# Rotary scores as two packed fp32r products, and casts moved behind head outputs

## The chip, the cores and the metric

The kernel runs on one core of a Trainium2 chip. The metric is the device time of one execution in microseconds (us), lower is better. A run of this kernel is compared with a run of the kernel before on the same chip. A profile of one execution tells what each engine did: TensorE (PE, with its weight loads shown apart as PEld), VectorE (DVE), ScalarE (ACT), GpSimd (POOL) and the DMA queues, most of which are issued by SyncE (SP).

## The reference

The program is a two-layer streaming encoder over 256 positions of width 1024, all in fp32. Each layer adds half a SwiGLU feed-forward (hidden width 2816), a token mixer, and half a second feed-forward. The mixer of layer 0 is a Conformer convolution, that of layer 1 is latent attention with 8 heads. The change touches the attention and, in three of the four feed-forwards, an order on two engines. What the attention computes:

```python
s = (jnp.einsum("bqhd,bkhd->bhqk", q_nope[:, q0:q1], k_nope[:, :q1])      # 128 numbers a head
     + jnp.einsum("bqhr,bkr->bhqk", q_rope[:, q0:q1], k_rope[:, :q1])     # 64 numbers, one key for all heads
     ) * scale
s = jnp.where(mask[None, None], s, -jnp.inf)                              # chunks of 64 positions
p = jax.nn.softmax(s, axis=-1)
outs.append(jnp.einsum("bhqk,bkhd->bqhd", p, v[:, :q1]))                  # blocks of 128 queries
```

So the first 128 queries see 128 keys and the last 128 queries see 256.

## The kernel before, in words

Positions are two tiles of 128 (`tb` or `qb`, 0 and 1). Nearly all weights pass through one pipeline: a block of 128 x 2048 fp32 numbers is fetched by SP into one of 4 `raw` buffers, ACT casts it to the shorter fp32r type (`hi`), DVE subtracts to get the rest (`lo`), in two pieces of 1024 columns each, and the pair stands in one of 5 weight buffers until PE has used it. A product is then three fp32r matmuls (`mm3`, lines 330 to 336): high by low, high by high, low by high. A few products are single fp32 matmuls instead, among them the scores, the transposes and probabilities by values; PE executes each of these as two records, except for a transpose, which is one.

The program is written as a list of operations, and a planner gives each engine its order from estimated times. Where the author wants another order, `order(a, b)` places `a` behind `b` without a wait of its own, `urgent` gives operations priority and records them, and `behind` places casts of weights behind the last few urgent operations of their engine. Each engine executes its list strictly in order.

The attention (`mla_in`, from line 1424) goes in this order: low-rank projections; the queries' rotary part (`qr`, lines 1529 to 1550), which DVE rotates into `qrope` with temporaries `rp`; the first four heads' query part `QN` (line 1552); transposes of the rotated key `kd` and of `qrope` (lines 1553 to 1562), whose results are copied into `KR` and `QR`; all heads' keys `KN`; the values `VV` (24 matmuls named `v`); the scores of heads 0, 1 and 2; the second four heads' `QN`; then a loop in which a head's scores (PE), softmax (DVE and ACT), transpose of its probabilities (PE, copied to `ptT` by ACT), its product with the values (`pv`, one PSUM bank) and its split into `Oh` (ACT) and `Ol` (DVE, both in `evicted`) overlap with the output projection `o`. The key is kept twice along the partitions, in two halves of 64, so that even and odd heads can share one tile; the 64 free rows of `KR` and `QR` hold -1e30 and 1 in such places that their product is the chunk mask. So the scores of a head are, for each of the two query tiles,

```python
nc.tensor.matmul(sc[qb], QN[:, hd, tbs(qb)], KN[:, hd, :n], start=True, stop=False)
last = nc.tensor.matmul(sc[qb], QR[:, hd % 2, hd // 2, tbs(qb)], KR[:, hd % 2, :n], start=False, stop=True)
```

with n = 128 or 256. The weights that are cast during the heads are the four blocks `wo` of the output projection and the first blocks `in_f2w` of the feed-forward that follows.

In a feed-forward, hidden columns are worked out in chunks `c` of 512; each ends in two groups (one for each position tile) whose result `s` is turned by way of DRAM (`turn`, line 846: DVE transposes `gt`, SP writes `gd` and reads it back into `rows` or `gb`) and split into `Gh` (ACT) and `Gl` (DVE); the pairs of these two casts are listed in `gates`. In the second, third and fourth feed-forward, chunk 3 is worked out with seven block products instead of eight (`seven_products`, line 368). Its seven weight blocks are made from four fetched ones by four DVE subtractions of 128 x 2048 (`load_seven`, line 189), and lines 395 to 404 say where the casts of the last two groups (those of chunk 2) stand among the casts of these blocks.

Of the kernel before, what the change touches and what calls it, by code (L numbers as in the profile page):

```python
# [11 lines left out]
F32 = mybir.dt.float32  # L12
# [77 lines left out]
def trunk(ctx: ExitStack, tc: tile.TileContext, x, xt, first, pos, invf, gfin, wdw,  # L90
# [71 lines left out]


    casts = {}

    turns = []
    last_read = [None]
# [21 lines left out]
    def load_seven(j, four, b, pieces):  # L189
        hi = wp.tile([P, HB], F32R, tag="hi", name=uid("hi"))  # L190
        lo = wp.tile([P, HB], F32R, tag="lo", name=uid("lo"))
        n = len(loaded)
        if j == 0:
            b[11], b[12] = fetched(four[0]), fetched(four[1])
        elif j == 1:
            b[22] = fetched(four[3])
        elif j == 2:
            b[21] = fetched(four[2])
        def sub(out, left, right):
            ins = nc.vector.tensor_sub(out, left, right)  # L200
            behind(ins)
            return ins

        if j == 1:
            sub(b[11], b[12], b[11])
            sub(b[12], b[22], b[12])
        elif j == 2:
            sub(b[11], b[22], b[11])
        elif j == 6:
            sub(b[11], b[21], b[11])  # L210
        raw = b[(11, 11, 11, 21, 12, 22, 11)[j]]
        for i in range(pieces):
# [155 lines left out]
    def seven_products(xh, xl, forms, banks, late={}):  # L368
# [22 lines left out]
        last = urgent(nc.scalar.copy)(kept, c22)  # L391
# [1011 lines left out]
    def rope(pool, dst, src, n, cc, sn, tb, after=()):  # L1403

        w = n * 64
        t1, t2 = (pool.tile([P, w], F32, tag=f"rp{w}", name=uid("rp"), bufs=3 if n > 1 else 4) for _ in range(2))
        a = t1[:, :w].rearrange("p (n i f) -> p n i f", i=2, f=32)
        b = t2[:, :w].rearrange("p (n i f) -> p n i f", i=2, f=32)
        full = [P, n, 2, 32]
        turned = [nc.vector.tensor_tensor(a, src, cc[:, tb, :, :].unsqueeze(1).to_broadcast(full), op=ALU.mult)]  # L1410
        for i in range(2):
            turned.append(nc.vector.tensor_tensor(b[:, :, i, :], src[:, :, 1 - i, :],
                                                  sn[:, tb, i, :].unsqueeze(1).to_broadcast([P, n, 32]), op=ALU.mult))
        for ins in turned:
            for first in after:
                order(ins, first.ins)
        nc.vector.tensor_add(dst, t1[:, :w], t2[:, :w])
# [6 lines left out]
    def mla_in(act, X, make_next, cc, sn):  # L1424
# [4 lines left out]
        CKl = act.tile([P, 2, S], F32R, tag="CKl", name="CKl")  # L1429


        KR = act.tile([P, 2, S], F32, tag="KR", name="KR")
        QR = act.tile([P, 2, H // 2, S], F32, tag="QR", name="QR")
        for x, fill in ((KR, -1e30), (QR, 1.0)):
            nc.gpsimd.memset(x, 0.0)
            for parity in range(2):
                for tb in range(NT):
                    row = 64 * (1 - parity) + 32 * tb
                    t = tb * P + (CHUNK if x is KR else 0)
                    nc.gpsimd.memset(x[row:row + 1, parity, ..., t:t + CHUNK], fill)  # L1440

        last_low = [None]

# [132 lines left out]

        score_last, maxima, powers, scaled = [], [], [], []

        def scores(hd):
            b = bank("B", "sc")  # L1580
            sc = {0: b[:, :P], 1: b[:, P:P + S]}
            for qb in range(NT):
                n = (qb + 1) * P
                nc.tensor.matmul(sc[qb], QN[:, hd, tbs(qb)], KN[:, hd, :n], start=True, stop=False)
                last = nc.tensor.matmul(sc[qb], QR[:, hd % 2, hd // 2, tbs(qb)], KR[:, hd % 2, :n], start=False,
                                        stop=True)
            score_last.append(last)
            return softmax(sc)

# [19 lines left out]
        def probs(pr):  # L1609
            b = transposed(pr, 0, 3)  # L1610
            pt = act.tile([P, 3 * P], F32, tag="ptT", name=uid("ptT"), bufs=2)
            nc.scalar.copy(pt, b[:, :3 * P])
            return pt

        def evicted(hd, b):
            nc.scalar.copy(Oh[:, hd, :], b[:, :S])
            nc.vector.tensor_sub(Ol[:, hd, :], b[:, :S], Oh[:, hd, :].bitcast(F32))

        def values(hd, pt):
            b = bank("C", "pv")  # L1620
            nc.tensor.matmul(b[:, :S], VV[:, 0, hd * VH:(hd + 1) * VH], pt[:, :S], start=True, stop=False)
            nc.tensor.matmul(b[:, P:S], VV[:, 1, hd * VH:(hd + 1) * VH], pt[:, S:], start=False, stop=True)
# [18 lines left out]
        nope(part, QN, 4, CQh, CQl, 512, 4, (0, 4), score_last[-1:])  # L1641
        o = Rows(Oh, Ol, H)
        for i in range(2, H + 3):
# [175 lines left out]
```

## Time and profile before

| what | value |
|---|---|
| median of 3 runs | 896.05 us (895.89 to 896.4) |
| the profiled execution | 896.07 us, its span 894.3 us |
| PE busy | 886.9 us, 99% of the span |
| PE weight loads | 745.9 us, 83% |
| DVE busy | 743.1 us, 83% |
| ACT busy | 571.8 us, 64% |
| POOL busy | 104.2 us, 12% |
| granted TensorE clock | 0.999 |
| matmul records of the scores | 64 in all, started between 666.3 and 691.6 us |

In the rows of the timeline the columns are start, length, engine, line, operation, tiles written and read, shape, and a count where equal instructions are merged; a bracket tells the idle time of the engine before it. The length of a matmul reaches over the start of the next, since matmuls are pipelined; the distance from one start to the next is what a matmul costs on PE.

### The profile page before, as it was taken

How to read it: one execution, taken by the hardware profiler on the slowest of the kernel's cores; microseconds unless marked ns; L12 is line 12 of the kernel's file. 1: busy time of each engine (PE TensorE's matmuls, PEld its weight loads, DVE VectorE, ACT ScalarE, POOL GpSimd, SP SyncE). 2: the span in 40 equal slices, each digit the busy share in tenths (PEclk: the TensorE clock that was granted, in tenths of full speed). 3: DMA queues.
4: the chain of work that ended last, by engine and by line, in shares of the span. 5: the costliest groups of instructions: out<-in, count | busy, mean ns of one | idle time of the engine just before them, and what ended most of it. 6: DMA issues, size and time to landing. Idle time of an engine off the chain costs nothing.

```text
span 894.3 us, 12241 instructions
## 1 busy us (share of the span) xinstructions
PE 886.9 (99%) x4221; PEld 745.9 (83%) x4221; DVE 743.1 (83%) x1083; ACT 571.8 (64%) x993; POOL 104.2 (12%) x227
## 2 busy tenths in 40 slices
PE   9999999999999999999999999999999999999997
PEld 7888888898988888888888888888899888888886
DVE  6787789579998999999588989995768579989973
ACT  7966458488886646667375566673677566474752
POOL 1000000069962000000010000001400010000000
PEclk9999999999999999999999999999999999999999
DMA  9987629834215864939759369495635349378541
GB/s 330 375 303 274 232 59 355 295 121 172 106 60 194 289 258 144 374 109 388 259 175 339 118 218 357 123 392 182 223 142 189 141 154 342 104 260 317 180 196 48
DMA packets 71055, 198.94 MB, mean 222 GB/s; under 512 B 12369, under 2 KB 41937, under 8 KB 51665
## 3 DMA queue, kind: packets, MB, share of 16 engines
q1 hardware_dynamic: 70560, 197.47, 61.8%
q8 instruction: 33, 0.54, 0.2%
q10 hardware_dynamic: 432, 0.69, 0.2%
q14 instruction: 30, 0.24, 0.1%
HBM read 181.87 MB, written 16.25 MB: 222 GB/s over the span
## 4 chain that ended last, share of the span: by engine, by line
PE 92%; DVE 4%; ACT 2%; DMA 1%; issue 0%; SPq 0%; POOL 0%; DVEq 0%; ACTq 0%
PE u L336 16%; PE u L335 16%; PE u L332 16%; PE o L335 9%; PE o L336 9%; PE o L332 9%; PE gate L1005 2%; PE u L411 2%; DVE acc L1094 2%; PE u L1005 2%; PE tp L446 1%; PE a L335 1%; PE a L332 1%; PE a L336 1%; PE nope L336 1%; PE nope L332 1%
## 5 line engine op out<-in xcount | busy, mean ns | idle before, releaser
L247 DVE TENSOR_TENSOR lo<-raw,hi 128x1024 fp32r<-128x1024 f32 (+1 forms) x236 | 276.2, 1212 | 38.8 <-ACT hi L246 37.6
L246 ACT CAST hi<-raw 128x1024 fp32r<-128x1024 f32 (+1 forms) x238 | 236.8, 1044 | 89.3 <-DMA raw<-in_f2w 30.8
L332 PE MATMUL u<-lo,Xh 128*128 128x512 f32 x612 | 238.4, 389 | 0.1
L336 PE MATMUL u<-hi,Xl 128*128 128x512 f32 x612 | 238.3, 389 | 0.0
L335 PE MATMUL u<-hi,Xh 128*128 128x512 f32 x612 | 238.1, 389 | 0.0
L332 PEld LDWEIGHTS u<-lo,Xh 128*128 128x128 f32 x612 | 114.9, 188 | 24.5 <-ACT Xh L598 0.5
L336 PEld LDWEIGHTS u<-hi,Xl 128*128 128x128 f32 x612 | 114.9, 188 | 24.3 <-DVE Xl L465 0.5
L335 PEld LDWEIGHTS u<-hi,Xh 128*128 128x128 f32 x612 | 114.9, 188 | 23.8
L214 ACT CAST hi<-raw 128x1024 fp32r<-128x1024 f32 x98 | 97.7, 1050 | 51.8 <-DVE raw L200 44.9
L200 DVE TENSOR_TENSOR lo<-raw,hi 128x1024 fp32r<-128x1024 f32 x98 | 115.6, 1216 | 7.1 <-ACT hi L214 7.1
L332 PE MATMUL o<-lo,Gh 128*128 128x512 f32 (+1 forms) x276 | 106.6, 386 | 0.0
L335 PE MATMUL o<-hi,Gh 128*128 128x512 f32 (+1 forms) x276 | 106.5, 386 | 0.0
L336 PE MATMUL o<-hi,Gl 128*128 128x512 f32 (+1 forms) x276 | 106.5, 386 | 0.0
L437 POOL TENSOR_TENSOR ms<-ss 128x1 f32<-128x1 f32 x16 | 8.1, 510 | 597.6 <-ACT junk L429 597.6
L200 DVE TENSOR_TENSOR raw<-raw,raw 128x2048 f32<-128x2048 f32 x28 | 63.9, 2283 | 1.8 <-DMA raw<-in_f2w 0.9
L332 PEld LDWEIGHTS o<-lo,Gh 128*128 128x128 f32 x276 | 51.8, 188 | 10.5
L335 PEld LDWEIGHTS o<-hi,Gh 128*128 128x128 f32 x276 | 51.9, 188 | 10.5
L336 PEld LDWEIGHTS o<-hi,Gl 128*128 128x128 f32 x276 | 51.8, 188 | 10.4
L1094 DVE SCALAR_TENSOR_TENSOR acc<-V,dw,acc 128x128 f32<-128x128 f32 (+1 forms) x174 | 53.9, 391 | 0.0
L1115 ACT ACTIVATE prod<-V,dw 128x128 f32<-128x128 f32 (+1 forms) x128 | 45.6, 415 | 1.8 <-POOL Y L1116 1.0
L956 ACT ACTIVATE s<-u,R 128x512 f32<-128x512 f32 (+1 forms) x48 | 30.9, 647 | 24.8 <-PE u L336 24.1
L797 DVE SCALAR_TENSOR_TENSOR h<-o,rh,h 128x512 f32<-128x512 f32 (+1 forms) x18 | 12.9, 719 | 29.2 <-PE o L336 29.2
(265 smaller groups left out, 1257.7 us busy)
## 6 DMA issues: line engine op xcount, KB each, us to landing
raw<-in_f2w SPq DMA_DIRECT2D x66, 1024.0 KB, 6.2
raw<-in_f1w SPq DMA_DIRECT2D x62, 1024.0 KB, 6.5
raw<-in_cw SPq DMA_DIRECT2D x12, 1024.0 KB, 5.5
gd<-gt SPq DMA_DIRECT2D x160, 64.0 KB, 3.0
gb<-gd SPq DMA_DIRECT2D x24, 256.0 KB, 2.8
rows<-gd SPq DMA_DIRECT2D x16, 256.0 KB, 4.4
raw<-in_wo SPq DMA_DIRECT2D x4, 1024.0 KB, 4.9
hd<-rows SPq DMA_DIRECT2D x56, 64.0 KB, 2.4
```

The source lines that it names most:

```text
L200: ins = nc.vector.tensor_sub(out, left, right)
L214: casts[n, i] = nc.scalar.copy(hi[:, c], raw[:, c]), sub(lo[:, c], raw[:, c], hi[:, c].bitcast(F32))
L246: casts[len(loaded), i] = (nc.scalar.copy(hi[:, c], raw[:, c]), low.tensor_sub(lo[:, c], raw[:, c], hi[:, c].bitcast(F32)))
L247: low.tensor_sub(lo[:, c], raw[:, c], hi[:, c].bitcast(F32)))
L332: mm = nc.tensor.matmul(o, ah, bl, start=start, stop=False, skip_group_check=seeded)
L335: nc.tensor.matmul(o, ah, bh, start=False, stop=False, skip_group_check=seeded)
L336: return nc.tensor.matmul(o, al, bh, start=False, stop=stop, skip_group_check=seeded)
L411: mm = nc.tensor.matmul(o, al if kind == "x" else ah, bl if kind == "l" else bh, start=start and n == 0, stop=stop and n == len(kinds) - 1)
L956: nc.scalar.activation(s[:, :w], u[0, tb][:, :w], AF.Silu, scale=X.r[tb])
L1005: mm = nc.tensor.matmul(u[:, t], w[:, c], X.x[:, k, t], start=(k == 0), stop=(k == KT - 1))
L1094: dve_last.append(nc.vector.scalar_tensor_tensor(out if j == j1 - 1 else y, v, w, y, op0=ALU.mult, op1=ALU.add))
L1115: prods_last.append(nc.scalar.activation(p, v, AF.Copy, scale=w))
```

## The change

- **Scores.** The rotary part is no longer one fp32 matmul but two fp32r matmuls. The key is cast to fp32r in `KA` (both halves), its rest goes to `KR`. The queries' high part stays in `QR`; a new tile `QA` for each parity and position tile holds the high part in one half and the rest in the other. `QA` by `KA` gives high by high and rest by high in one product; `QR` by `KR` gives high by rest, and the mask. The `QN` by `KN` product stays fp32. For the second query tile it is moved behind the fp32r ones, and all six are chained.
- **Making them.** For the key, 4 copies on ACT (64 x 128) become 2 copies on ACT (128 x 128) and 4 subtractions on DVE (64 x 128). For the queries, 2 copies on ACT and 2 on DVE (64 x 512) become 4 copies on ACT, 4 subtractions and 4 copies on DVE. The tiles of `QA` share the 6 buffers (before 3) of the rotation's temporaries. The products `v` are placed behind the transposes of `qrope`: those of the first output behind the first four transposes, the others behind the second four. The load of ACT's exponential table is placed behind the last copy into `QR`.
- **Casts during the heads.** The high casts of `wo` block 1 move from behind the third softmax to behind the first two copies into `ptT`; the casts of `wo` blocks 2 and 3 and of the next block are placed behind `Oh` and `Ol` of heads 1, 2 and 3; head 2's `evicted` becomes urgent.
- **Gates.** In `seven_products` the low casts of chunk 1's groups are placed behind the subtraction of the third of the seven blocks, and chunk 2's groups go later: their high casts behind those of the sixth and seventh block, their low casts behind the last low cast of the next plain block.

```diff
-            sub(b[11], b[22], b[11])
+            thirds[n] = sub(b[11], b[22], b[11])
...
-        for high, low in gates[-NT:] if not late else ():
-            order(high, last.ins)
-            order(low, add.ins)
-        low_gates = [low for high, low in gates[-NT:] if not late]
+        for high, low in gates[-2 * NT:-NT] if not late else ():
+            order(low, thirds[n0 + 2].ins)
+        late_gates = gates[-NT:] if not late else ()
...
-        for low in low_gates[1:]:
-            order(low, casts[n0 + 6, PIECES - 1][1].ins)
+        for n, (high, low) in enumerate(late_gates):
+            order(high, casts[n0 + 5 + n, PIECES - 1][0].ins)
+            order(low, casts[n0 + 7, PIECES - 1][1].ins)
...
-        t1, t2 = (pool.tile([P, w], F32, tag=f"rp{w}", name=uid("rp"), bufs=3 if n > 1 else 4) for _ in range(2))
+        t1, t2 = (pool.tile([P, w], F32, tag=f"rp{w}", name=uid("rp"), bufs=6 if n > 1 else 4) for _ in range(2))
...
+            nc.scalar.copy(KA[:, tbs(t)], b[:, :P])
             for i in range(2):
                 half = slice(64 * i, 64 * i + 64)
-                nc.scalar.copy(KR[half, i, tbs(t)], b[half, :P])
+                nc.vector.tensor_sub(KR[half, i, tbs(t)], b[half, :P], KA[half, tbs(t)].bitcast(F32))
+        turns_of = [], []
         for tb in range(NT):
-            b = transposed(qr[tb], 0, 4, (last,)).rearrange("p (j t) -> p j t", t=P)
-            for parity, copy in ((0, nc.scalar.copy), (1, nc.vector.tensor_copy)):
-                half = slice(64 * parity, 64 * parity + 64)
-                urgent(copy)(QR[half, parity, :, tbs(tb)], b[half])
+            b = transposed(qr[tb], 0, 4, (last,), turns_of[tb]).rearrange("p (j t) -> p j t", t=P)
+            for parity in range(2):
+                half, rest = (slice(64 * i, 64 * i + 64) for i in (parity, 1 - parity))
+                high = QR[half, parity, :, tbs(tb)]
+                turned_last = urgent(nc.scalar.copy)(high, b[half])
+                both = act.tile([P, 512], F32R, tag="rp512", name=uid("QA"), bufs=6).rearrange("p (j t) -> p j t", t=P)
+                urgent(nc.vector.tensor_sub)(both[rest], b[half], high.bitcast(F32))
+                urgent(nc.vector.tensor_copy)(both[half], high)
+                QA[parity, tb] = both
...
-                    mm3(b, CKh[:, k, tbs(tb)], CKl[:, k, tbs(tb)], hi[:, c], lo[:, c], k == 0, k == 1)
+                    mm3(b, CKh[:, k, tbs(tb)], CKl[:, k, tbs(tb)], hi[:, c], lo[:, c], k == 0, k == 1,
+                        turns_of[0][-1:] if (tb, d) == (0, 0) else turns_of[1][-1:])
...
-                nc.tensor.matmul(sc[qb], QN[:, hd, tbs(qb)], KN[:, hd, :n], start=True, stop=False)
-                last = nc.tensor.matmul(sc[qb], QR[:, hd % 2, hd // 2, tbs(qb)], KR[:, hd % 2, :n], start=False,
-                                        stop=True)
+                three = [(QN[:, hd, tbs(qb)], KN[:, hd, :n]), (QA[hd % 2, qb][:, hd // 2], KA[:, :n]),
+                         (QR[:, hd % 2, hd // 2, tbs(qb)], KR[:, hd % 2, :n])]
+                for i, (rows_of, keys) in enumerate(three if qb == 0 else three[1:] + three[:1]):
+                    mm = nc.tensor.matmul(sc[qb], rows_of, keys, start=i == 0, stop=i == 2)
+                    if last is not None:
+                        order(mm, last.ins)
+                    last = mm
...
+            if hd in (1, 2, 3):
+                for i in range(PIECES):
+                    for cast, first in zip(casts[len(loaded) - (2 if hd == 1 else 1), i], kept):
+                        order(cast, first.ins)
...
-            (urgent if hd in (3, 4, 5, 6) else lambda f: f)(evicted)(hd, b)
+            (urgent if hd in (2, 3, 4, 5, 6) else lambda f: f)(evicted)(hd, b)
...
+        order(table, turned_last.ins)
...
-        for j, i, highs, lows in ((0, 0, None, maxima[2]), (0, 1, None, scaled[0]), (1, 0, powers[2], scaled[1]),
-                                  (1, 1, powers[2], scaled[2])):
-            for cast, first in zip(casts[n_used[0] + j, i], (highs, lows)):
-                if first is not None:
-                    order(cast, first.ins)
+        for j, i, lows in ((0, 0, maxima[2]), (0, 1, scaled[0]), (1, 0, scaled[1]), (1, 1, scaled[2])):
+            high, low = casts[n_used[0] + j, i]
+            order(low, lows.ins)
+            if j == 1:
+                late.append(high)
...
+            if i < 4:
+                order(late[i - 2], copies[-1].ins)
```

More of the change, by code (lines that the diff above doesn't have):

```diff
@@ L164, in trunk @@
     casts = {}
+    thirds = {}
     turns = []
@@ L390, in seven_products @@
         kept = tmp.tile([P, 512], F32, tag="s", name=uid("p5"))
-        last = urgent(nc.scalar.copy)(kept, c22)
+        urgent(nc.scalar.copy)(kept, c22)
         product(forms[1], c21, False)
@@ L1429, in mla_in @@
         CKl = act.tile([P, 2, S], F32R, tag="CKl", name="CKl")
-        KR = act.tile([P, 2, S], F32, tag="KR", name="KR")
-        QR = act.tile([P, 2, H // 2, S], F32, tag="QR", name="QR")
+        KA = act.tile([P, S], F32R, tag="KA", name="KA")
+        QA = {}
+        KR = act.tile([P, 2, S], F32R, tag="KR", name="KR")
+        QR = act.tile([P, 2, H // 2, S], F32R, tag="QR", name="QR")
         for x, fill in ((KR, -1e30), (QR, 1.0)):
-            nc.gpsimd.memset(x, 0.0)
+            nc.gpsimd.memset(x.bitcast(F32), 0.0)
             for parity in range(2):
@@ L1439, in mla_in @@
                     t = tb * P + (CHUNK if x is KR else 0)
-                    nc.gpsimd.memset(x[row:row + 1, parity, ..., t:t + CHUNK], fill)
+                    nc.gpsimd.memset(x[row:row + 1, parity, ..., t:t + CHUNK].bitcast(F32), fill)
         last_low = [None]
@@ L1575, in mla_in @@
         Ol = act.tile([P, H, S], F32R, tag="CQ", name="Ol")
-        score_last, maxima, powers, scaled = [], [], [], []
+        score_last, maxima, powers, scaled, copies, late = [], [], [], [], [], []
         def scores(hd):
@@ L1581, in scores @@
             sc = {0: b[:, :P], 1: b[:, P:P + S]}
+            last = None
             for qb in range(NT):
                 n = (qb + 1) * P
-                nc.tensor.matmul(sc[qb], QN[:, hd, tbs(qb)], KN[:, hd, :n], start=True, stop=False)
-                last = nc.tensor.matmul(sc[qb], QR[:, hd % 2, hd // 2, tbs(qb)], KR[:, hd % 2, :n], start=False,
-                                        stop=True)
+                three = [(QN[:, hd, tbs(qb)], KN[:, hd, :n]), (QA[hd % 2, qb][:, hd // 2], KA[:, :n]),
[5 more added lines that the diff above has]
+                    last = mm
             score_last.append(last)
@@ L1611, in probs @@
             pt = act.tile([P, 3 * P], F32, tag="ptT", name=uid("ptT"), bufs=2)
-            nc.scalar.copy(pt, b[:, :3 * P])
+            copies.append(nc.scalar.copy(pt, b[:, :3 * P]))
             return pt
         def evicted(hd, b):
-            nc.scalar.copy(Oh[:, hd, :], b[:, :S])
-            nc.vector.tensor_sub(Ol[:, hd, :], b[:, :S], Oh[:, hd, :].bitcast(F32))
+            kept = (nc.scalar.copy(Oh[:, hd, :], b[:, :S]),
+                    nc.vector.tensor_sub(Ol[:, hd, :], b[:, :S], Oh[:, hd, :].bitcast(F32)))
+            if hd in (1, 2, 3):
+                for i in range(PIECES):
+                    for cast, first in zip(casts[len(loaded) - (2 if hd == 1 else 1), i], kept):
+                        order(cast, first.ins)
         def values(hd, pt):
```

## The prediction

> **What bounds the kernel now.** I read the page first, then the scores in PE's timeline, then PE's gaps around them, then what DVE, ACT and SP do beside them.
>
> ```profile
> span 894.3 us, 12241 instructions
> PE 886.9 (99%) x4221; PEld 745.9 (83%) x4221; DVE 743.1 (83%) x1083; ACT 571.8 (64%) x993; POOL 104.2 (12%) x227
> PE 92%; DVE 4%; ACT 2%; DMA 1%; issue 0%; SPq 0%; POOL 0%; DVEq 0%; ACTq 0%
> ```
>
> PE is busy for 99% of the span and holds 92% of the chain that ended last. So a microsecond taken from PE is a microsecond of the time, unless a wait appears in its place; work added to DVE or ACT is free as long as PE does not wait for it. But a matmul's length overlaps the next one's, so I cost PE by distances between starts. A head's scores stand alone here:
>
> ```profile
> 676.02 0.49 PE L446 MATMUL tp<-ident,pr 128*128 128x128 f32 x3
> 676.35 0.39 PE L1584 MATMUL sc<-KN,QN 128*128 128x128 f32 x2
> 676.57 0.39 PE L1585 MATMUL sc<-KR,QR 128*128 128x128 f32 x2
> 676.79 0.60 PE L1584 MATMUL sc<-KN,QN 128*128 128x256 f32 x2
> 677.23 0.59 PE L1585 MATMUL sc<-KR,QR 128*128 128x256 f32 x2
> 677.66 0.49 PE L446 MATMUL tp<-ident,pr 128*128 128x128 f32 x3
> 677.99 0.60 PE L1621 MATMUL pv<-ptT,VV 128*128 128x256 f32 x2
> 678.42 0.38 PE L1622 MATMUL pv<-ptT,VV 128*128 128x128 f32 x2
> ```
>
> From 676.35 to 677.66 a head takes 1.31 us: an fp32 product (two records) costs 0.22 over 128 columns and 0.435 over 256.
>
> **Scores: what is removed and added on PE.** Two fp32 products a head (0.22 + 0.435 = 0.655 us) give way to four fp32r ones, two over 256 columns and two over 128. These rows price the first pair and the change of type:
>
> ```profile
> 659.72 0.28 PE L335 MATMUL nope<-CKh,hi 128*128 128x256 f32 x1
> 659.84 0.29 PE L336 MATMUL nope<-CKh,lo 128*128 128x256 f32 x1
> 659.96 0.60 PE L446 MATMUL tp<-ident,qrope 128*128 128x128 f32 x4
> 660.32 0.47 PE L332 MATMUL v<-lo,CKh 128*128 128x512 f32 x1
> 660.63 0.39 PE L335 MATMUL v<-hi,CKh 128*128 128x512 f32 x1
> 660.85 0.39 PE L336 MATMUL v<-hi,CKl 128*128 128x512 f32 x1
> ```
>
> An fp32r product over 256 columns costs 0.12 us (659.72 to 659.84), over 512 about 0.225 (660.63 to 660.85). From the first transpose to the second `v` is 0.67 us, and four transposes at 0.11 (three take 0.33 at 676.02) with one `v` make 0.665: going from fp32 to fp32r costs nothing that can be read here, and going back (0.12 from 659.84 to 659.96) nothing either. I put 0.01 us on a head for both.
>
> No row shows an fp32r product over 128 columns. From below: fp32r costs 0.225 at 512, 0.12 at 256, and 0.1465 at 320 (the next two rows are the first and the last of 21 in a run, 2.93 us over 20 distances), so 0.0004 us a column, which is 0.067 at 128. From above: the fp32 pair, 0.22. Between them stand operations that have one weight load and hardly any streaming:
>
> ```profile
> 638.72 0.31 PE L332 MATMUL a<-lo,Xh 128*128 128x320 f32 x1
> ...
> 641.65 0.31 PE L336 MATMUL a<-hi,Xl 128*128 128x320 f32 x1
> ...
> 249.97 1.17 PE L1132 MATMUL ms<-ones,sq 128*128 128x1 f32 x10
> 251.00 0.47 PE L1241 MATMUL o<-lo,Zh 128*128 128x512 f32 x1
> 251.32 0.39 PE L1241 MATMUL o<-hi,Zh 128*128 128x512 f32 x1
> ...
> L335 PEld LDWEIGHTS nope<-CQ,hi 128*128 128x128 f32 x32 | 6.1, 192 | 0.0
> L1584 PEld LDWEIGHTS sc<-KN,QN x32: 187/192/192, 666.1 to 691.0; 128*128 128x128 f32 x32
> ```
>
> Ten `ms` records over a single column and the `o` behind them take 1.35 us, so 0.112 each: that is no streaming, it is the rate at which weights are loaded. The load of an fp32r operand (192 ns) is as long as that of an fp32 one (192), and the transposes too come at 0.11. So I take 0.11 for a product over 128 columns, the row it is nearest to.
>
> A head then costs 0.655 + 2 x 0.12 + 2 x 0.11 + 0.01 = 1.125, which saves 0.185 us; eight heads save **1.48 us**. The ends: at 0.067 they save 2.17 us, at 0.22 they lose 0.28 us.
>
> The Trainium skill has a rule at odds with this row: "TensorE: Matmul & The Clock Gate", section "Weight-path perf modes — Fast Weight Load (FWL) and DoubleRow", says that loads of 128 weights go about twice as fast where the type is not fp32. The equal loads of 192 ns above speak against that for fp32r. The same page's "Back-to-back issue gap" gives some 81 ns for a load and a product over 128 columns, by which the saving would be an estimated 1.94 us; nothing of that kind is shown in this trace.
>
> **Casts behind head outputs.** What could these moves win? PE's distances between the heads exceed those of 676 to 678 us in one place:
>
> ```profile
> 686.04 2.35 DVE L247 TENSOR_TENSOR lo<-raw,hi 128x1024 fp32r<-128x1024 f32 x2
> ...
> 688.38 0.42 DVE L1617 TENSOR_TENSOR Ol<-pv,Oh 128x256 fp32r<-128x256 f32 x1
> ...
> 688.48 0.49 PE L446 MATMUL tp<-ident,pr 128*128 128x128 f32 x3
> 688.85 0.70 PE L1621 MATMUL pv<-ptT,VV 128*128 128x256 f32 x2
> 689.39 0.38 PE L1622 MATMUL pv<-ptT,VV 128*128 128x128 f32 x2
> ```
>
> The three transposes take 0.37 instead of 0.33 and the `pv` pair 0.54 instead of 0.43: 0.15 us. `pv` has one PSUM bank; head 1's `Ol`, done at 688.80, frees it, and stood behind two casts of weights. With those casts behind head 1's outputs the wait goes: **0.15 us** saved. What is late next is those casts. They belong to `wo` blocks 2 and 3, which PE reads after 699 us; a shift of some 5 us is covered. The high casts of `wo` block 1 go from 672.4 to about 677 and 679 (ACT's first `ptT` copies), and that block is read from about 692. If the cover is gone, PE waits up to 2.35 us, the two casts of one block. SP gets no new DMA, but raw buffers come free up to some 5 us later, so loads of `in_f2w` are issued later, and what stands behind them on SP's queue as well: the turned rows of the next norm, at 715.5 in SP's queue, are held by DVE's work of 714.8 and have some 5 us in hand behind the last load, which I count as enough.
>
> **Making `KA`, `KR`, `QR` and `QA`.** DVE gains 4 subtractions of 64 x 128 (about 0.28 each, between the 0.26 that ACT takes and the 0.34 of a 128 x 128 split), 4 of 64 x 512 and 4 copies less 2 (0.694 each by the row of the old copy): 1.1 + 2.8 + 1.4 = 5.3 us. ACT gains 0.6 (4 x 0.58 and 2 x 0.26 less 2 x 0.58 and 4 x 0.26). Nothing in this stage makes PE wait for DVE, and DVE is idle between its last rotation and the first softmax:
>
> ```profile
> L258 DVE COPY QR<-tp 64x512 f32<-64x512 f32 x2 | 1.4, 694 | 5.8 <-ACT QR L258 5.8
> ...
> 658.67 0.69 DVE L1417 TENSOR_TENSOR qrope<-rp,rp 128x512 f32<-128x512 f32 x1
> 661.25 0.69 DVE L258 COPY QR<-tp 64x512 f32<-64x512 f32 x1 [1.90 <-ACT QR L258]
> 665.80 0.69 DVE L258 COPY QR<-tp 64x512 f32<-64x512 f32 x1 [3.86 <-ACT QR L258]
> 668.73 1.15 DVE L1597 TENSOR_REDUCE nm<-sc 128x1 f32<-128x128 f32 x4 [2.23 <-PE sc L1585]
> ...
> 664.51 0.60 PE L446 MATMUL tp<-ident,qrope 128*128 128x128 f32 x4
> 666.34 0.38 PE L1584 MATMUL sc<-KN,QN 128*128 128x128 f32 x2
> ```
>
> That is 1.90 + 3.86 + 2.23 = 8.0 us for 4.2 (the other 1.1 comes earlier, beside casts). The second transposes of `qrope` move from 664.5 to about 661.7, behind the first six `v`. ACT's two copies end by about 663.5, DVE's two subtractions and copies by about 665.8. The first scores start at 666.3; the last tile of `QA` is for odd heads, so it is not read before head 1, over 1 us later. I count this as **0**. The `v` products themselves cost the same in another order.
>
> **Gates.** No PE gap stands in these stages, so nothing can be won; the moves could only cost. In the second feed-forward:
>
> ```profile
> 357.38 0.69 DVE L853 TENSOR_TENSOR Gl<-gb,Gh 128x512 fp32r<-128x512 f32 x1
> ...
> 359.71 3.49 DVE L247 TENSOR_TENSOR lo<-raw,hi 128x1024 fp32r<-128x1024 f32 x3
> ...
> 360.82 0.39 PE L332 MATMUL u<-lo,Xh 128*128 128x512 f32 x1
> ```
>
> The next plain block's second low cast, the first of the three from 359.71, ends about 360.9, just as PE comes to it at 360.82. With the 0.69 us `Gl` behind it, it comes earlier. What is late then is that `Gl`, and with it its `gb` buffer, which the next turn needs at 372: 11 us in hand. **0**.
>
> **Sum.** 1.48 + 0.15 = 1.63 us off. The profiled execution took 896.07 us (span 894.3), 0.02 above the median of 896.05; from that median the forecast is **894.4 us**.
>
> **The rivals.** What this kernel's measurement can tell from no change is about 0.2%, 1.8 us; the bounds are 894.26 and 897.84.
>
> *A. Short fp32r products go at the column rate.* If the weight load hides, 0.067 each and 2.17 + 0.15 off: 893.7 us. For it: 256, 320 and 512 columns lie on one line, with no sign of a floor at 0.12. Against: the equal loads, the 0.11 of the transposes. The fast loads that the Trainium skill's page of above tells of would make this case.
>
> *B. PE waits for the second `qrope` (the other side).* The 18 `v` behind the second transposes now queue behind them, where before they ran ahead of them (664.51). The rotation ended at 659.36, 2.3 us ahead of 661.7, and the key's subtractions take 1.1 of that. If one more block's low casts (2.35) get ahead, PE waits 1.1 us; with two blocks, 3.5 us: 896.05 - 1.63 + 3.5 = 897.9 us. It decides from 3.4 us of PE wait on. Against: six buffers instead of three let the second rotation start sooner.
>
> *C. Short fp32r products go no faster than fp32.* At 0.22 the change does not do what it says: 896.05 + 0.28 - 0.15 = 896.2 us, no change. Against: that is twice the load's rate.
>
> *D. The saving is returned.* PE reaches the next feed-forward 1.6 us sooner while casts for it have been moved later; one cast (1.2 us) in PE's way leaves 895.6 us.
>
> **How the numbers follow.** Forecast 0.42, within 894.0 to 895.2; A 0.22; B 0.13; C 0.11; D 0.12. Faster by over 0.2% is A and about a quarter of the forecast's spread: 0.33. Slower is B: 0.13. The rest, 0.54, is within 0.2%. The range leaves out B and a little of A: 893.4 to 896.7 us.
>
> **What would show it.** A head's scores at 1.1 us from start to start (1.04 for A, 1.35 for C), with the short fp32r products at 0.11; the six `v` and the transposes at 661.7 without a gap (a gap is B); no `pv` pair over 0.43; the next feed-forward starting 1.6 us sooner than 713.4, and the end sooner by the same (less is D). The prediction is wrong if PE shows new gaps, or if short products cost something else than a weight load.

## The result and the profile after

| | before | after |
|---|---|---|
| median (22 runs each, taken together) | 896.87 us (895.27 to 900.12) | 894.43 us (893.82 to 897.01) |
| ratio after to before | | 0.9975, 95% interval 0.9968 to 0.9981 |
| profiled execution, its span | 896.07 us, 894.3 us | 894.99 us, 893.2 us |

By the ratio 2.2 us were saved, with an interval of 1.7 to 2.9 us; between the medians lie 2.44 us. The forecast had been a saving of 1.63 us from a median of 896.05. With more runs the median of the kernel before stands at 896.87, so that 894.4 and 894.43 agree better than the savings do. That the two times meet is luck: the kernel before came out 0.82 us slower than the median that I started from, and the saving 0.81 us larger than forecast.

The head of the page and its chain, after:

```profile
span 893.2 us, 12273 instructions
PE 885.5 (99%) x4221; PEld 744.1 (83%) x4221; DVE 746.7 (84%) x1093; ACT 571.6 (64%) x993; POOL 104.9 (12%) x227
PE 94%; DVE 2%; DMA 2%; issue 1%; ACT 0%; SPq 0%; POOL 0%; DVEq 0%; ACTq 0%
```

PE still bounds the kernel. DVE took 3.6 us more work, without a price that shows here. The same head as before the change, in PE's timeline of after:

```profile
676.01 0.49 PE L447 MATMUL tp<-ident,pr 128*128 128x128 f32 x3
676.33 0.39 PE L1602 MATMUL sc<-KN,QN 128*128 128x128 f32 x2
676.48 0.30 PE L1602 MATMUL sc<-KA,QA 128*128 128x128 f32 x1
676.62 0.28 PE L1602 MATMUL sc<-KR,QR 128*128 128x128 f32 x1
676.73 0.33 PE L1602 MATMUL sc<-KA,QA 128*128 128x256 f32 x1
676.90 0.28 PE L1602 MATMUL sc<-KR,QR 128*128 128x256 f32 x1
677.02 0.59 PE L1602 MATMUL sc<-KN,QN 128*128 128x256 f32 x2
677.45 0.49 PE L447 MATMUL tp<-ident,pr 128*128 128x128 f32 x3
...
687.74 0.59 PE L1644 MATMUL pv<-ptT,VV 128*128 128x256 f32 x2
688.17 0.38 PE L1645 MATMUL pv<-ptT,VV 128*128 128x128 f32 x2
```

From 676.33 to 677.45 the head takes 1.12 us, where it took 1.31. Inside the head the starts lie 0.15, 0.14, 0.11, 0.17, 0.12 and 0.43 us apart; the first of these is less than the 0.22 that the same fp32 product took before, so the price of a product is not read from one such distance but from the whole head. The `pv` pair at 687.74 takes 0.43 us to the next; in the kernel before, the one at 688.85 took 0.54.

A single execution's span moves by more than a microsecond for reasons elsewhere, so I measure the stage itself: from the start of the first projection matmul `a` to the start of the last low product of `o`. These are its two ends, first in the kernel before:

```profile
623.38 0.39 PE L332 MATMUL a<-lo,Xh 128*128 128x512 f32 x1
...
712.29 0.48 PE L332 MATMUL o<-lo,Oh 128*128 128x512 f32 x1
```

and in the kernel after:

```profile
623.97 0.39 PE L333 MATMUL a<-lo,Xh 128*128 128x512 f32 x1
...
711.24 0.48 PE L333 MATMUL o<-lo,Oh 128*128 128x512 f32 x1
...
712.37 0.48 PE L333 MATMUL u<-lo,Xh 128*128 128x512 f32 x1
```

That is 88.91 us before and 87.27 after: **1.64 us saved in the attention**. The same distance in all kernels that were run (in another run of the changed kernel it came to the same 87.27):

| kernel | attention, us | against before |
|---|---|---|
| before | 88.91 | |
| gates alone (two runs) | 88.92, 88.88 | 0 |
| scores alone | 88.88 | -0.03 |
| casts alone | 88.75 | -0.16 |
| all but the casts | 88.89 | -0.02 |
| all but the gates (two runs) | 87.30, 87.27 | -1.61, -1.64 |
| all (two runs) | 87.27, 87.27 | -1.64 |
| all, short products widened | 87.34 | -1.57 |
| all, more changes of type | 87.20 | -1.71 |
| all, `v` in free order | 88.43 | -0.48 |
| all, only `wo` block 1's casts moved | 89.24 | +0.33 |

What is left of the 2.2 us, 0.1 to 1.2 us by its interval, lies outside the attention. There, every engine's instructions stand in the same order in the profiles of scores alone, casts alone and the kernel before, so of the parts of the change only the gates can matter in it.

### The profile page after: what moved, and what is told of

It is laid out like the page before. It is cut to its first block, busy times and chain, and to the rows that moved or that the text cites. A ratio compares the mean times of both kernels' runs of the same rounds, so it can differ in the third digit from the quotient of the medians.

```text
span 893.2 us, 12273 instructions
## 1 busy us (share of the span) xinstructions
PE 885.5 (99%) x4221; PEld 744.1 (83%) x4221; DVE 746.7 (84%) x1093; ACT 571.6 (64%) x993; POOL 104.9 (12%) x227
## 4 chain that ended last, share of the span: by engine, by line
PE 94%; DVE 2%; DMA 2%; issue 1%; ACT 0%; SPq 0%; POOL 0%; DVEq 0%; ACTq 0%
PE u L337 15%; PE u L333 15%; PE u L336 15%; PE o L337 9%; PE o L333 9%; PE o L336 9%; PE u L1006 3%; PE gate L1006 3%; PE u L412 2%; PE o L1242 2%; DMA raw<-in_f2w 2%; PE sc L1602 1%; PE tp L447 1%; DVE lo L201 1%; PE pairs L1049 1%
```

## The experiments

**The gates alone.** The kernel before, with nothing but the new order of the gates' casts:

```diff
...
-        for high, low in gates[-NT:] if not late else ():
-            order(high, last.ins)
-            order(low, add.ins)
-        low_gates = [low for high, low in gates[-NT:] if not late]
+        for high, low in gates[-2 * NT:-NT] if not late else ():
+            order(low, thirds[n0 + 2].ins)
+        late_gates = gates[-NT:] if not late else ()
...
-        for low in low_gates[1:]:
-            order(low, casts[n0 + 6, PIECES - 1][1].ins)
+        for n, (high, low) in enumerate(late_gates):
+            order(high, casts[n0 + 5 + n, PIECES - 1][0].ins)
+            order(low, casts[n0 + 7, PIECES - 1][1].ins)
```

> The kernel before with the order of the gates' casts alone changed. The prediction counted 0 for it: 896.9 us beside 896.9 of before, ratio 1.000. Rival (the measured gain of 2.4 us is larger than the 1.63 of scores and casts because the new order gives the weights' casts some hand in the stages with seven products): about 0.8 us off, ratio 0.999.

Measured: 896.0 us, ratio 0.9985 (0.9976 to 0.9995). The attention is unmoved at 88.92. So some 1.3 us (0.4 to 2.2) were saved by a part that I had counted at nothing.

**Scores alone.** The kernel before, with the three products of the scores, what makes their tiles, the order of `v` and the table's load; no cast of weights and no gate is moved:

```diff
...
-                nc.tensor.matmul(sc[qb], QN[:, hd, tbs(qb)], KN[:, hd, :n], start=True, stop=False)
-                last = nc.tensor.matmul(sc[qb], QR[:, hd % 2, hd // 2, tbs(qb)], KR[:, hd % 2, :n], start=False,
-                                        stop=True)
+                three = [(QN[:, hd, tbs(qb)], KN[:, hd, :n]), (QA[hd % 2, qb][:, hd // 2], KA[:, :n]),
+                         (QR[:, hd % 2, hd // 2, tbs(qb)], KR[:, hd % 2, :n])]
...
```

> The kernel before with the scores alone changed (and the making of KA, QA, KR, QR with the order of the v products and of the table load); casts and gates as before. The prediction: 1.48 us off, ratio 0.9983, a head at 1.12 us from start to start, no gap before the second transposes of qrope. The 0.15 us gap at a pv may stay. Rival: all of the 2.4 us is here, ratio 0.9973.

Measured: 897.0 us, ratio 0.9995 (0.9985 to 1.0006), and the attention 0.03 us shorter: nearly nothing, although each head's scores are cheaper. One new wait takes the saving. The kernel's list of waits has it (total, times, longest):

```profile
PEld pv L1639 <- ACT ptT L1630: 1.5, 1, 1.5
```

The first product with the values waits for the transposed probabilities; the next experiment shows the same wait from ACT's side.

**Everything but the casts.** The changed kernel with the casts of weights in their old places:

```diff
-            if hd in (1, 2, 3):
-                for i in range(PIECES):
-                    for cast, first in zip(casts[len(loaded) - (2 if hd == 1 else 1), i], kept):
-                        order(cast, first.ins)
...
-            if i < 4:
-                order(late[i - 2], copies[-1].ins)
```

> The changed kernel without the moved casts during the heads. The prediction: 0.15 us lost against the changed kernel, a gap of 0.1 to 0.2 us at one pv among the heads. Rival: with PE ahead by 0.2 us a head, the casts that stand in front of a head's outputs cost more than before, 0.5 us or more.

Measured: 895.95 us, ratio 0.9986 (0.9976 to 0.9996); the attention is at 88.89, as before the change: not 0.15 but 1.62 us are lost against the changed kernel. ACT's timeline in this kernel:

```profile
675.51 2.00 ACT L247 CAST hi<-raw 128x1024 fp32r<-128x1024 f32 x2
677.40 0.60 ACT L1531 COPY QN<-nope 128x512 f32<-128x512 f32 x1
677.88 0.89 ACT L1631 COPY ptT<-tp 128x384 f32<-128x384 f32 x2
```

and PE's:

```profile
676.72 0.49 PE L447 MATMUL tp<-ident,pr 128*128 128x128 f32 x3
...
678.44 0.70 PE L1640 MATMUL pv<-ptT,VV 128*128 128x256 f32 x2 [1.23 <-ACT ptT L1631]
```

The transposes start at 676.72, but the copy into `ptT` begins only at 677.88, behind the two high casts of `wo` block 1 (2.00 us), which stand on ACT behind the third softmax. Why was that harmless in the kernel before? ACT's and DVE's timelines there:

```profile
672.29 0.23 ACT L1600 ACTIVATION_READ_ACCUMULATOR pr<-sc,nm 128x1 f32 x1
672.38 2.02 ACT L246 CAST hi<-raw 128x1024 fp32r<-128x1024 f32 x2
...
676.70 0.48 ACT L1612 COPY ptT<-tp 128x384 f32<-128x384 f32 x1
...
670.47 0.62 DVE L1597 TENSOR_REDUCE nm<-sc 128x1 f32<-128x128 f32 x2 [0.38 <-PE sc L1585]
671.01 0.16 DVE L1603 RECIPROCAL sm<-sm 128x2 f32<-128x2 f32 x1
```

and in the kernel after:

```profile
676.14 0.21 ACT L1619 ACTIVATION_READ_ACCUMULATOR pr<-sc,nm 128x1 f32 x1
...
676.70 0.51 ACT L1631 COPY ptT<-tp 128x384 f32<-128x384 f32 x1
677.07 1.09 ACT L247 CAST hi<-raw 128x1024 fp32r<-128x1024 f32 x1
...
667.02 0.42 DVE L259 CAST QA<-QR 64x512 fp32r<-64x512 f32 x1
...
671.72 0.17 DVE L1622 RECIPROCAL sm<-sm 128x2 f32<-128x2 f32 x1 [2.21 <-ACT pr L1619]
671.80 1.13 DVE L1616 TENSOR_REDUCE nm<-sc 128x1 f32<-128x128 f32 x4
```

Before, DVE took all three heads' maxima and only then head 0's reciprocal; the third softmax left ACT at 672.5, and the casts ended at 674.4, long ahead of `ptT`. After, head 0's reciprocal stands in front of the maxima of heads 1 and 2 on DVE and waits 2.21 us for ACT; the third softmax ends at 676.35, 3.8 us later (of which 0.6 us is that the whole stage starts later in this execution). Casts behind it would now meet the `ptT` copies. In the full change they stand behind these copies (677.07), and PE loses nothing. The planner wrote the new order on DVE. That it did so because the last `QA` ends late (667.44, where I had put it at 665.8) is only argued. The order of `v` is not the cause: without it (below, `v` in free order) the reciprocal at 671.78 still stands ahead of the four maxima at 673.58. Whether it is the added work on DVE and ACT or the place of the table's load was not tested apart.

**Casts alone.** The kernel before, with all the moved casts and head 2's `evicted` urgent:

```diff
+            if hd in (1, 2, 3):
+                for i in range(PIECES):
+                    for cast, first in zip(casts[len(loaded) - (2 if hd == 1 else 1), i], kept):
+                        order(cast, first.ins)
...
-            (urgent if hd in (3, 4, 5, 6) else lambda f: f)(evicted)(hd, b)
+            (urgent if hd in (2, 3, 4, 5, 6) else lambda f: f)(evicted)(hd, b)
...
+            if i < 4:
+                order(late[i - 2], copies[-1].ins)
```

> The kernel before with the moved casts during the heads alone. The prediction: 0.15 us off, attention 88.76 instead of 88.91 us, ratio 0.9998. Rival (these moves are worth 1.6 us whatever the scores, as their removal from the changed kernel cost that): attention 87.3 us, ratio 0.998.

Measured: 897.24 us, ratio 0.9998 (0.9988 to 1.0009). The attention is 0.16 us shorter, which is the 0.15 of the forecast; so small a gain cannot be told in the whole time. Alone, the scores bring 0.03 and the casts 0.16; together they bring 1.64.

**Only the casts of `wo` block 1.** The changed kernel, with the two high casts behind the `ptT` copies, but the later casts not held behind `Oh` and `Ol`:

```diff
-            if hd in (1, 2, 3):
-                for i in range(PIECES):
-                    for cast, first in zip(casts[len(loaded) - (2 if hd == 1 else 1), i], kept):
-                        order(cast, first.ins)
...
-            (urgent if hd in (2, 3, 4, 5, 6) else lambda f: f)(evicted)(hd, b)
+            (urgent if hd in (3, 4, 5, 6) else lambda f: f)(evicted)(hd, b)
```

> The changed kernel with only the first of the moved casts (the high casts of wo block 1 behind the copies into ptT); those behind heads' outputs and head 2's priority are as before the change. Without all moved casts, pv waited 1.5 us for ptT, whose copy stood behind the two high casts of that block on ACT. Theory: this move alone takes the 1.5 us away, and the 0.15 us at head 1's output stays: attention 87.4 us. Rival: the copy then stands behind another cast, and 0.5 us or more of the wait stays.

Measured: 896.09 us in a single run; the attention takes 89.24, longer than with no cast moved. The wait for `ptT` is gone, as expected, but a larger one has come that neither theory nor rival had. ACT's timeline, then PE's, then the wait:

```profile
681.76 3.88 ACT L247 CAST hi<-raw 128x1024 fp32r<-128x1024 f32 x4
685.54 0.37 ACT L1635 CAST Oh<-pv 128x256 fp32r<-128x256 f32 x1
...
685.97 0.50 PE L333 MATMUL o<-lo,Oh 128*128 128x512 f32 x1 [0.73 <-ACT Oh L1635]
...
PEld o L333 <- ACT Oh L1635: 2.0, 2, 1.1
```

Four casts run in one piece, and the `Oh` that PE needs next stands behind them. At head 2's `Oh`, the same happens with two casts at 689.78: 2.0 us in two waits. So the casts have to move together: with none moved a wait of 1.5 us is left, with only these one of 2.0 us. The later casts moved without these were not run.

**`v` in free order.** The changed kernel without the order of `v` behind the transposes of `qrope`:

```diff
-                    mm3(b, CKh[:, k, tbs(tb)], CKl[:, k, tbs(tb)], hi[:, c], lo[:, c], k == 0, k == 1,
-                        turns_of[0][-1:] if (tb, d) == (0, 0) else turns_of[1][-1:])
+                    mm3(b, CKh[:, k, tbs(tb)], CKl[:, k, tbs(tb)], hi[:, c], lo[:, c], k == 0, k == 1)
```

> The changed kernel without the order of the v products behind the transposes of qrope; the planner puts the second transposes where they were before, behind 18 of the 24 products, 2.7 us later. The work on QA for the second tile then ends 2.7 us later, at about 670 us, behind the first scores. Theory: cover is gone, PE waits 0.5 to 2 us at the scores or later at the first pv. Rival: the planner finds other work for PE and the attention stays at 87.3 us.

Measured: 895.55 us in a single run; the attention 1.16 us longer than with the order. In PE's timeline:

```profile
667.20 0.60 PE L1601 MATMUL sc<-KN,QN 128*128 128x256 f32 x2
668.27 0.46 PE L1601 MATMUL sc<-KN,QN 128*128 128x128 f32 x2 [0.47 <-DVE QA L259]
```

Here the scores wait for `QA`. From 667.20 to 668.27 are 1.07 us, where such a product takes 0.435, so some 0.64 of the 1.16 us are lost at this place; by the list of waits, PE's weight loads also wait 0.4 us for an `Oh` that they do not wait for in the changed kernel. So the making of `QA` is hidden in the changed kernel because its transposes were pulled ahead of 18 `v`. There PE comes to them without a gap, 0.23 us after the last `v` before them:

```profile
662.14 0.39 PE L337 MATMUL v<-hi,CKl 128*128 128x512 f32 x1
662.37 0.60 PE L447 MATMUL tp<-ident,qrope 128*128 128x128 f32 x4
```

**Short products widened.** The changed kernel with all fp32r products of the scores over 256 columns, those of the first query tile too. The extra columns go to a part of the bank that nobody reads; the fp32 product stays at 128. The edit also moves the fp32 product behind the other two in the first query tile, as it already stands in the second:

```diff
-            sc = {0: b[:, :P], 1: b[:, P:P + S]}
+            sc = {0: b[:, :P], 1: b[:, S:]}
...
-                three = [(QN[:, hd, tbs(qb)], KN[:, hd, :n]), (QA[hd % 2, qb][:, hd // 2], KA[:, :n]),
-                         (QR[:, hd % 2, hd // 2, tbs(qb)], KR[:, hd % 2, :n])]
-                for i, (rows_of, keys) in enumerate(three if qb == 0 else three[1:] + three[:1]):
-                    mm = nc.tensor.matmul(sc[qb], rows_of, keys, start=i == 0, stop=i == 2)
+                three = [(QN[:, hd, tbs(qb)], KN[:, hd, :n]), (QA[hd % 2, qb][:, hd // 2], KA),
+                         (QR[:, hd % 2, hd // 2, tbs(qb)], KR[:, hd % 2, :])]
+                for i, (rows_of, keys) in enumerate(three[1:] + three[:1]):
+                    to = sc[qb] if i == 2 else b[:, qb * S:qb * S + S]
+                    mm = nc.tensor.matmul(to, rows_of, keys, start=i == 0, stop=i == 2)
```

> The changed kernel with the two fp32r products of the first query tile over 256 columns instead of 128 (the further columns are never read). If a short product costs a weight load, as the prediction took it (0.11 us), doubling its columns costs 0.01 each: a head's scores go from 1.12 to 1.14 us. If it costs its columns (rival A, 0.067 us), a head goes up by 0.107 us. The attention, from the first matmul a to the last o of Oh, 87.27 us in the changed kernel, becomes 87.4 by the first and 88.1 by the second.

Measured: 895.44 us in a single run; the attention 0.07 us longer. A head in PE's timeline:

```profile
676.16 0.49 PE L447 MATMUL tp<-ident,pr 128*128 128x128 f32 x3
...
676.61 0.28 PE L1603 MATMUL sc<-KR,QR 128*128 128x256 f32 x1
...
677.62 0.49 PE L447 MATMUL tp<-ident,pr 128*128 128x128 f32 x3
```

From transposes to transposes a head takes 1.46 us, and 1.44 in the changed kernel (676.01 to 677.45). Twice the columns cost 0.01 us a product. At the column rate of rival A, two products of 0.067 would have become two of 0.12: 0.106 a head, 0.85 in all. So over 128 columns it is not the columns that are paid. That the floor is the weight load is read from the `ms` records, which come 0.112 apart over a single column.

**More changes of type.** The changed kernel with the fp32 product first for both query tiles, so that PE goes between fp32 and fp32r more often:

```diff
-                for i, (rows_of, keys) in enumerate(three if qb == 0 else three[1:] + three[:1]):
+                for i, (rows_of, keys) in enumerate(three):
```

> The changed kernel with the fp32 product first in the second query tile too, so that a head has three turns between the types more or less instead of one: fp32, two fp32r, fp32, two fp32r. The prediction put 0.01 us on all turns of a head: the attention stays within 0.1 us of 87.27. Rival (the turn from fp32 to fp32r costs the 0.08 us by which the first fp32r product's distance is longer): 8 heads x 0.08 = 0.6 us more.

Measured: 893.62 us in a single run; the attention 0.07 us shorter. A head:

```profile
675.02 0.39 PE L1602 MATMUL sc<-KN,QN 128*128 128x128 f32 x2
...
676.13 0.49 PE L447 MATMUL tp<-ident,pr 128*128 128x128 f32 x3
```

It takes 1.11 us with two more turns of type. Such turns cost nothing that can be read here, and the place of the fp32 product in the second tile brings nothing either.

**Everything but the gates, twice; the changed kernel again; the gates alone again.** The edit of the first two is the gates' diff of above, taken back; the others have no new edit.

> The changed kernel without the new order of the gates' casts. The prediction: nothing lost, 1.63 us off before, ratio 0.9982. Rival (gates give 0.8 us): ratio 0.9982 too, but the changed kernel itself is at 0.9973, so this one is 0.8 us slower than that; if the gates give nothing, it is at 0.9973 like the changed kernel.

> The changed kernel without the new order of the gates' casts, once more. Theory (the gates' order gives the weights' casts in the stages with seven products some hand when a transfer comes late): gaps of some 0.1 to 0.4 us near the last of the seven blocks or the next plain block (357 to 360 us in the first profile), and a time 0.4 to 1 us above the changed kernel's. Rival (nothing): no such gap, the same time within 0.3 us.

> The changed kernel once more, beside the other runs of this call: ratio 0.9975 as measured. Its attention at 87.27 us. Theory: gaps outside the attention (at about 262, 398, 406 and 452 us in the first profile) come and go from one execution to the next, so they stand elsewhere or are missing here. Rival: they are of the new order and stand in the same places.

> The kernel before with the order of the gates' casts alone changed, once more. Theory: 0.4 to 1.1 us off (ratio 0.9988 to 0.9995). Rival: ratio 1.000 within 0.0003.

Measured, each against the kernel before on its own chip:

| kernel | median, us | ratio to before | interval |
|---|---|---|---|
| all but the gates | 895.22 | 0.9971 | 0.9959 to 0.9983 |
| all but the gates, again | 895.73 | 0.9981 | 0.9972 to 0.9991 |
| all, again | 895.27 | 0.9979 | 0.9970 to 0.9988 |
| gates alone | 896.0 | 0.9985 | 0.9976 to 0.9995 |
| gates alone, again | 896.72 | 0.9990 | 0.9981 to 0.9998 |

On the kernel before, the gates save 1.3 and 0.9 us, and both intervals exclude nothing saved. Scores alone and everything but the casts differ by the gates and by nothing else: 897.0 and 895.95 us on one chip, 1.05 us. On top of the rest the gates save 0.46 us on another chip (895.73 to 895.27) and cannot be told from zero by these intervals; the first run without them, at 0.9971, is no worse than the whole change. What they can win is shown in the fourth feed-forward of the second run without them, by ACT, DVE and PE:

```profile
792.67 0.62 ACT L853 CAST Gh<-gb 128x512 fp32r<-128x512 f32 x1 [2.34 <-DMA gb<-gd]
...
790.55 2.29 DVE L200 TENSOR_TENSOR raw<-raw,raw 128x2048 f32<-128x2048 f32 x1
...
793.77 1.98 ACT L214 CAST hi<-raw 128x1024 fp32r<-128x1024 f32 x2
...
794.84 2.36 DVE L200 TENSOR_TENSOR lo<-raw,hi 128x1024 fp32r<-128x1024 f32 x2 [0.26 <-ACT hi L214]
...
795.29 0.40 PE L336 MATMUL u<-hi,Gl 128*128 128x512 f32 x1
796.13 0.50 PE L332 MATMUL u<-lo,Xh 128*128 128x512 f32 x1 [0.44 <-DVE lo L200]
```

ACT stands for 2.34 us at `Gh`, whose turned rows have not landed; behind it are one activation and the high casts of the seventh block, behind these DVE's low casts, and PE comes 0.84 us after its last start where 0.23 is usual. DVE had made the seventh block by 792.84 (790.55 + 2.29); its high cast starts 0.93 us later. In the changed kernel `Gh` stands behind these casts:

```profile
791.41 2.00 ACT L215 CAST hi<-raw 128x1024 fp32r<-128x1024 f32 x2 [1.58 <-DVE raw L201]
793.32 0.61 ACT L854 CAST Gh<-gb 128x512 fp32r<-128x512 f32 x1
```

The same was seen in the second feed-forward in the first run without the gates, whose ACT waited 1.83 us:

```profile
354.49 0.62 ACT L853 CAST Gh<-gb 128x512 fp32r<-128x512 f32 x1 [1.83 <-DMA gb<-gd]
...
357.38 0.19 PEld L332 LDWEIGHTS u<-lo,Xh 128*128 128x128 f32 x1 [0.42 <-DVE lo L200]
```

How long ACT stands there depends on when the transfer lands, which varies from run to run. The view of the tile `Gh` tells for what ACT sat idle before it; in the kernel before and then in the one after it says

```profile
  DMA gb<-gd: 14.7, 10
```

```profile
  DMA gb<-gd: 9.3, 5
```

The two numbers are us and times; without the gates again and in the changed kernel again it is 20.0 us (11 times) and 8.4 us (5). Over all fourteen profiles it is 14.7 to 20.0 us with the old order and 6.5 to 9.3 us with the new one. How much of this reaches PE can be read too, since outside the attention PE's matmuls come in the same order in all fourteen profiles. From the matmul that starts at 785.01 us in the kernel before to the one at 801.80, in the fourth feed-forward, it is 16.77 us in all nine profiles with the new order; with the old order it is 16.79 in three, 17.05 in scores alone and 17.91 in the second run without the gates. Around the same place of the second feed-forward (340.17 to 364.90) it is 24.71 us in all nine; with the old order 24.73 in four, and 25.17 in the first run without the gates. So the new order does take this loss away: 0.04 us in the profile of before, up to 1.2 us in others, 0.4 us on average of the five. That is less than most of the differences between medians; where the rest comes from, or whether there is one, no run shows.

As for the gaps that the third of the four texts asks about: of the changed kernel's first profile, those at 262 and 452 us stand in its second profile as well, and those at 398 and 406 do not. Two like those at 262 and 452 stand in casts alone too, where the gates have the old order, so these are not of the new order.

## Why the prediction was right, and where not

- **Scores, 1.48 us.** A head went from 1.31 to 1.12 us; 1.125 was forecast. The short product is (1.12 - 0.655 - 0.24 - 0.01) / 2 = 0.11 us, as taken from the `ms` records, and the widened products confirm that it does not go by its columns. Rivals A (0.067) and C (0.22) are refuted. By the Trainium skill's "TensorE: Matmul & The Clock Gate", "LDWEIGHTS (loading the stationary operand)", a load of 128 columns takes an estimated 107 ns (128 / 1.2). The 0.11 from start to start agrees with this; the records of the loads themselves last 187 to 192 ns. The faster loads that the Trainium skill gives on the same page for types that aren't fp32 ("Weight-path perf modes — Fast Weight Load (FWL) and DoubleRow") and its 81 ns ("Back-to-back issue gap") do not show for fp32r: with them a product over 256 columns would have cost clearly more than one over 128, and it cost 0.01 more.
- **Changes of type, 0.01 a head.** Nothing can be read: 1.11 us with two more turns.
- **Casts, 0.15 us.** Alone 0.16: the term is right by itself. But as a part of the change it was sized wrongly, because the next point failed.
- **Making the tiles, "I count this as 0".** This step failed. It asked only whether PE waits for `QA`, and PE doesn't. It didn't ask what the planner would do with DVE's and ACT's order after it: the softmax of heads 1 and 2 ends 3 to 4 us later, and with the old places of the casts PE waits 1.5 us for `ptT`. So the part of the change that makes the tiles isn't free: left so, it costs the whole saving of the scores. Which of its edits turned the order on DVE stays open, except that the order of `v` did not. This is rival D's mechanism in another place, and with the casts on the other side: moving them was not what might return the saving, but what kept it. The sum of 1.63 still came out (1.64), and that is luck: the casts were moved for a wait of 0.15 us, and kept away one of 1.5 us that the prediction did not see. Both parts were in the change: on top of the moved casts the scores bring 1.48 us (88.75 to 87.27), without them 0.02 or 0.03; the casts bring 0.16 alone and 1.62 on top of the scores (88.89 to 87.27). Costing the casts at 0.15 was costing them beside the old scores.
- **Rival B.** PE shows no gap at the second transposes, now at 662.37. The order of `v` is needed: without it the attention is 1.16 us longer.
- **Gates, "No PE gap stands in these stages, so nothing can be won".** Wrong as a conclusion. It was true of the one execution that I had (896.07 us, below the median of 896.87). In others the transfer comes later, and the old order lets ACT's wait for it delay casts for PE. By the pairs of medians on one chip it is worth 0.5 to 1.3 us, by the profiles 0.04 to 1.2 us an execution; more closely it stays open.
- **The end.** The next feed-forward starts 88.40 us after the first `a` (712.37 less 623.97), and 90.04 before (713.42 less 623.38): 1.64 us sooner, as the forecast said (1.6), and nothing is given back. The whole saving is larger than forecast, and the gates are the likely rest, though not shown to be all of it: the first measurement (1.7 to 2.9) hardly leaves room for 1.63 alone, the second, 1.9 us (1.1 to 2.7), does.
- **The chances.** 0.54 was given to no change that can be told and 0.33 to faster. The saving of 0.25% (0.19 to 0.32%) lies just over the bound of 0.2%, and its interval reaches below it.

## What to carry to other kernels

A cheaper product wins its time only if the work that makes its operands doesn't reorder the engines behind it: after such a change look at what stands ahead of the next copy or cast on each in-order engine, since a long cast of weights that was harmless may now be in front of what the bounding engine needs. Here an edit that won 0.03 us alone, and another that won 0.16 us alone, won 1.64 together; test parts both alone and left out. And one execution without gaps doesn't show that a wait for a transfer is harmless: move such a wait behind the work that does not need it, and compare many runs.

## What was new about the hardware

- An fp32r product costs 0.11 us over 128 columns and 0.12 over 256: between these two hardly anything is won by making it shorter, while an fp32 product goes from 0.435 to 0.22.
- PE goes back and forth between fp32 and fp32r products at no cost that can be read (1.11 us a head against 1.12).
- DVE copies 64 x 512 fp32r numbers within SBUF in 0.42 us, while the subtraction that reads PSUM takes 0.69 and the old copy out of PSUM took 0.69 as well; I had counted all at 0.69. DVE's busy time rose by 3.6 us, not 5.3.
- ACT and DVE stand still at an instruction that waits (2.34 us at `Gh`, 2.21 at the reciprocal), and what is behind it waits too. The Trainium skill says in "TensorE: Matmul & The Clock Gate", "Architectural detail: the array is 16× 32×32, not 1× 128×128", that these two are strict FIFO (first in, first out), and the trace agrees. What was new is how much the waits of one kernel differ between runs. Of the changed kernel's two profiles the first lists a wait of 0.5 us of PE's weight loads in a feed-forward, for turned rows, and the second does not.
